# Two of four feed-forward half steps of a decoder in seven block products for eight

## The chip, the cores and the metric

One core of one Trainium2 chip runs the whole program, in one launch. The metric is device time in microseconds (us), the median of three runs. The engines are TensorE (PE in the profile; PEld is its load of weights), VectorE (DVE), ScalarE (ACT), GpSimd (POOL) and SyncE (SP), which here only issues transfers. TensorE multiplies out of SBUF into PSUM, which has eight banks of 2 KB on each of 128 partitions.

## What is computed

The trunk has two layers, 544 tokens (512 of a prompt and 8 x 4 of a sample group), a model width of 1024 and a feed-forward width of 2816. Each layer has a feed-forward half step, a mixer (an mLSTM in layer 0, a chunk MLP in layer 1) and a second half step; a norm ends it. All is float32.

```python
def _swiglu(x, w_gate, w_up, w_down):
    return (jax.nn.silu(x @ w_gate) * (x @ w_up)) @ w_down
...
    for i in range(DEPTH):
        x = x + 0.5 * _swiglu(_rmsnorm(x, p['norm_ff1'][i]),
                              p['ffn1_w_gate'][i], p['ffn1_w_up'][i], p['ffn1_w_down'][i])
...
        x = x + out
        x = x + 0.5 * _swiglu(_rmsnorm(x, p['norm_ff2'][i]),
                              p['ffn2_w_gate'][i], p['ffn2_w_up'][i], p['ffn2_w_down'][i])
    y = _rmsnorm(x, p['norm_final'])
```

The half steps are called ffn1,0, ffn2,0, ffn1,1 and ffn2,1 here, in the order of their running.

## The kernel before, in words

Features lie on the partitions: x is eight tiles of 128 x 544, and a weight is used in pieces of 128 x 1024, eight blocks of 128 x 128 that make one tile of 128 outputs. The tokens go in two halves of 272 columns, one PSUM bank each.

A float32 product is three products of a narrower format (float32r). Each operand is split exactly into a part `hi` and a part `lo` (`split_into`): ScalarE copies it into the narrower format (`whi` for weights, `hh` for the hidden activations, `xgh` for x), VectorE subtracts that copy from it (`wlo`, `hl`, `xgl`). `mm3` then adds hi times hi, hi times lo and lo times hi for every k block and both halves: 48 matmuls for eight k blocks, all recorded at L191. `whi` and `wlo` have two buffers each, the loaded pieces (`raw`) six.

A half step (`ffn`) takes the 22 hidden tiles in groups of 8, 8 and 6 (`FF_GROUPS`). For each hidden tile j it makes the gate product, then the up product; VectorE multiplies the gate by the norm's factors (L277), ScalarE takes Silu (L278), GpSimd multiplies by the factors again (L279), VectorE multiplies by the up product (L180), and the result is split into `hh` and `hl`. Behind a group come eight down products of 48 or 36 matmuls, each added to one tile of x (L294). In the last group of a half step each new x tile is at once scaled, split and squared for the next norm (`prep`); the squares are added up by GpSimd (L234). `prep_end` turns the sum into the norm's factors `rstd` through TensorE, a square root on ScalarE (L245) and a reciprocal on VectorE (L246). The program's last group goes through `last_down` (its products of the last tile at L319, its update of x at L323) and `finish`, the final norm.

At the start the x tiles and the first piece of weights come in, interleaved; the splits of x go ahead of the squares, which VectorE adds, and the factors are made behind the first two products.

The order on each engine is made by a list scheduler when the program is built; each engine then works its queue strictly in that order, and waits on semaphores of the others. Weights are issued by SP, one transfer of 512 KB for a piece.

## Time and profile before

| what | us |
|---|---|
| median of three runs | 2337.63 (2336.07 to 2338.55) |
| span of the profiled execution, first to last instruction | 2334.9 |
| TensorE busy | 2314.8 (99%) |
| VectorE busy | 1126.5 (48%) |
| ScalarE busy | 787.8 (34%) |
| GpSimd busy | 351.5 (15%) |

A time of the runs holds what lies ahead of the first and behind the last instruction too, so it stands 2.7 us above the span. A busy time is the length of all instructions of an engine with overlaps counted once; matmuls overlap each other, so the mean length of one (288 ns) is over twice the distance from one to the next.

### The profile page before, as it was taken

To read this page: it belongs to the slowest core of one execution; us is meant where nothing else is said; L and a number is where in the kernel's file an instruction comes from. 1 tells how busy PE (TensorE), PEld (TensorE's weight loads), DVE (VectorE), ACT (ScalarE), POOL (GpSimd) and SP (SyncE) were. 2 spreads that over 40 slices of the span, in tenths; PEclk is the share of its full clock that TensorE was granted. 3 is DMA by queue.
4 is the path that set the end of the run, shared out by engine and by line. 5 is a ranking of instruction groups with operands and counts; after the bars stand their busy time and mean duration, and the time that the engine had idled before them with its cause. 6 is when DMAs were issued, how large, how long until landed. Compare 5 with 4: busy or idle time off the path is not lost.

```text
span 2334.9 us, 42078 instructions
## 1 busy us (share of the span) xinstructions
PE 2314.8 (99%) x18076; PEld 2220.8 (95%) x18076; DVE 1126.5 (48%) x1642; ACT 787.8 (34%) x1066; POOL 351.5 (15%) x403
## 2 busy tenths in 40 slices
PE   8999999999999999999999999999999999999998
PEld 8999999988987789999999999999999999999998
DVE  5333336543456676644454454545444644333334
ACT  5222123434455453422222342122233433222123
POOL 1101013332111100210111121011121121001011
PEclk9999999999999999999999999999999999999999
DMA  5322223467767663547563444746333223223221
GB/s 179 90 83 91 91 76 110 152 223 233 247 214 259 237 192 102 173 157 265 157 212 118 139 148 157 264 157 210 119 102 96 70 82 91 90 83 91 91 71 59
DMA packets 131089, 337.50 MB, mean 145 GB/s; under 512 B 13168, under 2 KB 26304, under 8 KB 130904
## 3 DMA queue, kind: packets, MB, share of 16 engines
q1 hardware_dynamic: 101152, 276.52, 36.7%
q0 software_dynamic: 9200, 34.02, 4.5%
q10 hardware_dynamic: 20552, 24.29, 2.9%
q8 instruction: 142, 2.33, 0.4%
q14 instruction: 43, 0.35, 0.0%
HBM read 274.97 MB, written 59.81 MB: 143 GB/s over the span
## 4 chain that ended last, share of the span: by engine, by line
PE 95%; DVE 2%; DMA 2%; ACT 1%; issue 0%; POOL 0%; SPq 0%; DVEq 0%; ACTq 0%
PE mm L191 83%; PE mm L926 2%; PE s L191 2%; PE s L719 1%; PE s L497 1%; PE s L853 1%; PE s L889 1%; PE s L1110 1%; DMA xs<-xsd 1%; DMA raw<-in_ml_down 1%; PE s L1040 0%; PE s L836 0%; DVE wlo L206 0%; PE s L478 0%; DVE wg L424 0%
## 5 line engine op out<-in xcount | busy, mean ns | idle before, releaser
L205 ACT ACTIVATE whi<-raw 128x1024 fp32r<-128x1024 f32 (+2 forms) x345 | 358.0, 1038 | 1296.1 <-PE mm L191 1114.4
L191 PE MATMUL mm<-xgh,whi 128*128 128x272 f32 x3744 | 779.7, 289 | 5.8 <-ACT whi L205 5.8
L191 PE MATMUL mm<-xgl,whi 128*128 128x272 f32 x3744 | 776.1, 288 | 0.4 <-DVE xgl L209 0.4
L191 PE MATMUL mm<-xgh,wlo 128*128 128x272 f32 x3744 | 775.1, 288 | 0.0
L191 PEld LDWEIGHTS mm<-xgh,whi 128*128 128x128 f32 x3744 | 588.3, 188 | 23.8 <-issue 14.1
L191 PEld LDWEIGHTS mm<-xgl,whi 128*128 128x128 f32 x3744 | 587.8, 188 | 0.7 <-DVE xgl L209 0.6
L191 PEld LDWEIGHTS mm<-xgh,wlo 128*128 128x128 f32 x3744 | 587.4, 188 | 0.5 <-issue 0.5
L206 DVE TENSOR_TENSOR wlo<-raw,whi 128x1024 fp32r<-128x1024 f32 (+2 forms) x345 | 413.5, 1199 | 63.0 <-ACT whi L205 49.2
L191 PE MATMUL mm<-hh,whi 128*128 128x272 f32 x1508 | 314.2, 289 | 1.3 <-DVE x L294 1.3
L191 PE MATMUL mm<-hl,whi 128*128 128x272 f32 x1508 | 312.2, 288 | 0.0
L191 PE MATMUL mm<-hh,wlo 128*128 128x272 f32 x1508 | 312.0, 288 | 0.1
L279 POOL TENSOR_TENSOR s<-s,rstd 128x544 f32<-128x544 f32 x88 | 151.8, 1726 | 1002.5 <-ACT s L278 1002.5
L191 PEld LDWEIGHTS mm<-hh,whi 128*128 128x128 f32 x1508 | 236.2, 188 | 6.2 <-issue 6.1
L191 PEld LDWEIGHTS mm<-hh,wlo 128*128 128x128 f32 x1508 | 236.5, 188 | 0.8 <-DVE wlo L206 0.8
L191 PEld LDWEIGHTS mm<-hl,whi 128*128 128x128 f32 x1508 | 236.8, 188 | 0.0
L180 DVE TENSOR_TENSOR t<-mm,s 128x544 f32<-128x544 f32 x83 | 60.1, 725 | 331.6 <-PE mm L191 331.6
L294 DVE SCALAR_TENSOR_TENSOR x<-mm,x 128x544 f32<-128x544 f32 x88 | 63.7, 724 | 249.1 <-PE mm L191 249.1
L277 DVE TENSOR_TENSOR t<-mm,rstd 128x544 f32<-128x544 f32 x88 | 63.6, 724 | 240.5 <-PE mm L191 240.4
L1114 DVE SCALAR_TENSOR_TENSOR c<-c,gib,s 128x512 f32<-128x512 f32 x128 | 88.1, 740 | 0.0
L234 POOL TENSOR_TENSOR acc<-acc,sq 128x544 f32<-128x544 f32 x35 | 56.5, 1614 | 175.7 <-ACT sq L233 175.7
L206 DVE TENSOR_TENSOR hl<-t,hh 128x544 fp32r<-128x544 f32 x88 | 63.2, 718 | 2.9 <-ACT hh L205 2.9
L1116 POOL DMA_DIRECT2D out_Cs<-c x32 | 25.0, 782 | 253.4 <-DVE c L1114 246.6
(304 smaller groups left out, 1763.1 us busy)
## 6 DMA issues: line engine op xcount, KB each, us to landing
raw<-in_ffn_up SPq DMA_DIRECT2D x88, 512.0 KB
raw<-in_ffn_gate SPq DMA_DIRECT2D x87, 512.0 KB
raw<-in_ffn_down SPq DMA_DIRECT2D x64, 512.0 KB
c<-in_sC SPq DMA_DIRECT2D x64, 512.0 KB
c<-in_sC SPq DMA_DIRECT2D x32, 1024.0 KB
out_Cs<-c POOLq DMA_DIRECT2D x32, 1024.0 KB, 6.0
raw<-in_ml_up SPq DMA_DIRECT2D x32, 512.0 KB
raw<-in_ffn_down SPq DMA_DIRECT2D x32, 384.0 KB
```

The source lines that it names most:

```text
L180: self.nc.vector.tensor_tensor(out=self.v2(out), in0=ps[:, :, :HN], in1=self.v2(by), op=ALU.mult)
L191: nc.tensor.matmul(out=ps[h], lhsT=w[:, wsl], rhs=x[:, h * HN:(h + 1) * HN], start=k == 0 and q == 0, stop=k == n - 1 and q == 2)
L205: nc.scalar.activation(out=hi, in_=src, func=AF.Copy)
L206: nc.vector.tensor_tensor(out=lo, in0=src, in1=hi.bitcast(F32), op=ALU.subtract)
L234: (eng or nc.gpsimd).tensor_tensor(out=self.acc, in0=self.acc, in1=sq, op=ALU.add)
L277: nc.vector.tensor_tensor(out=self.v2(t), in0=psg[:, :, :HN], in1=self.v2(self.rstd), op=ALU.mult)
L279: nc.gpsimd.tensor_tensor(out=s, in0=s, in1=self.rstd, op=ALU.mult)
L294: nc.vector.scalar_tensor_tensor(out=xv, in0=ps[:, :, :HN], scalar=0.5, in1=xv, op0=ALU.mult, op1=ALU.add)
L497: nc.tensor.matmul(out=ps[:, tt * P:(tt + 1) * P], lhsT=t[:, tt * P:(tt + 1) * P], rhs=wd[w], start=True, stop=True)
L926: nc.tensor.matmul(out=ps, lhsT=kk[:, tt], rhs=vv[:, tt], start=tt == 0 and q == 0, stop=tt == 3 and q == 2)
L1114: nc.vector.scalar_tensor_tensor(out=c0[:, r, :], in0=c0[:, r, :], scalar=self.gib[:, h, b:b + 1], in1=ps[r], op0=ALU.mult, op1=ALU.add)
L1116: nc.gpsimd.dma_start(out=self.pair(o["Cs"], v)[:, h, dsl].rearrange("r p e -> p r e"), in_=c0)
```

## The change

ffn1,0 and ffn2,1 use the scheme of Strassen and Winograd. A weight is cut into blocks of 2 x 2: two neighbouring k tiles by two neighbouring output tiles; the tokens' two halves are the second matrix's columns. Seven products of block sums then stand for eight of blocks. `sums` makes the sums of x (once) or of the hidden activations on VectorE, in a tile of eight slots of 272 columns (`hT`), and splits seven of them. `weight_sums` loads the four blocks of a weight's piece once, in four transfers of 256 KB, and forms four sums: two on GpSimd (L396, L399), two on VectorE (L397, L398). It splits the seven blocks in three pieces of 128 x 1024 (`whi`, `wlo`, as before with two buffers) and one of 128 x 512 (`whd`, `wld`, one buffer).

`seven` makes the products in four PSUM banks of one tile `set` (two such tiles, all eight banks), P1 to P7 in the order of the code: P1 in bank 0, P2 in bank 1, P3 on bank 2, P4 on bank 0, P5 on bank 3, P6 on bank 2, P7 on bank 1. Between them ScalarE carries a bank's content to another: L425 behind P1 (bank 0 to bank 2, negated), L428 behind P2 (bank 1 to SBUF, `e`), L430 behind P3 (bank 2 to bank 3), L433 behind P5 (bank 3 to bank 1, negated). A product has 12 matmuls of 272 columns in a gate or up seven; in a down seven it has 9, or 6 in the last group, since the hidden tiles go in pairs, in groups of three, three, three and two (`SV_GROUPS`). All these matmuls are recorded at L421. A gate seven is followed by L458 to L460 on VectorE, Silu of 1088 columns (L461) and a product on GpSimd of 1088 columns (L462), an up seven by L467, L469 and L470 and the sums of the hidden pair (L353, L355, L356, then the split of 1904 columns into `hh` and `hl` at L241 and L242), a down seven by L493, L495 and L496, which add to two tiles of x.

The program has 72 sevens: 44 for gate and up, 28 for down. The last group of ffn2,1 goes through a rewritten `last_down` in the old scheme, with 24 matmuls a tile. At the start all of x is summed and split pair by pair through one buffer of `hT`, and GpSimd adds the squares. The middle stages keep their code; their buffers are grouped otherwise (`x_pool`, `psum`).

```diff
+SEVEN = {("ffn1", 0), ("ffn2", 1)}
+SV_GROUPS = ((0, 3), (3, 6), (6, 9), (9, 11))
+ADDS = "eng"
+B11, B21, B22, T4, T1, T2, T3, B12 = range(8)
...
     def prep(self, k):
+        if self.xkind == "s":
+            if k % 2:
+                self.px[k // 2] = self.sums_x(k - 1)
+            self.prep_sq(k)
+            return
...
+    def set(self):
+        return self.pp.tile([P, 4, 512], F32, tag="set", name="set", bufs=2)
+
+    def sums(self, t, hi, lo, parts=1):
+
+        nc = self.nc
+        nc.vector.tensor_tensor(out=t[:, T1:T3 + 1:2], in0=t[:, B12:B12 + 1].to_broadcast([P, 2, HN]),
+                                in1=t[:, B11:B22 + 1:2], op=ALU.subtract)
+        nc.vector.tensor_tensor(out=t[:, T2], in0=t[:, B22], in1=t[:, T1], op=ALU.subtract)
+        nc.vector.tensor_tensor(out=t[:, T4], in0=t[:, B21], in1=t[:, T2], op=ALU.subtract)
+        for c in ((slice(0, 7),) if parts == 1 else (slice(0, 3), slice(3, 7))):
+            self.split_into(hi[:, c], lo[:, c], t[:, c])
+        return hi, lo
+
+    def sums_x(self, k):
+
+        nc = self.nc
+        t = self.ht.tile([P, 8, HN], F32, tag="hT", name="hT", bufs=1)
...
+        return self.sums(t, hi, lo, 2)
+
+    def weight_sums(self, src):
...
+        ta, tb, tc = (raw(self.wp, "raw", 2, RAW) for _ in range(3))
+        td = raw(self.wx, "rawd", 1, 2)
+        nc.sync.dma_start(out=ta[:, 0], in_=b11)
...
+            t21 = raw(self.wx, "raw21", 1, 1)
+            nc.sync.dma_start(out=t21[:, 0], in_=b21)
+            nc.sync.dma_start(out=tc[:, 0], in_=b22)
+            nc.sync.dma_start(out=tb[:, 0], in_=b12)
+            nc.gpsimd.tensor_tensor(out=ta[:, 1], in0=ta[:, 0], in1=t21[:, 0], op=ALU.add)
+            nc.vector.tensor_tensor(out=tc[:, 1], in0=tc[:, 0], in1=t21[:, 0], op=ALU.add)
+        nc.vector.tensor_tensor(out=tb[:, 1], in0=tc[:, 1], in1=ta[:, 0], op=ALU.add)
+        nc.gpsimd.tensor_tensor(out=td[:, 0], in0=tb[:, 1], in1=tb[:, 0], op=ALU.add)
+        out = []
+        for t in (ta, tb, tc):
+            hi, lo = (self.wp.tile([P, 2, 512], F32R, tag=g, name=g, bufs=WSP)[:, :, :n] for g in ("whi", "wlo"))
+            self.split_into(hi, lo, t)
+            out += [(hi[:, i], lo[:, i]) for i in range(2)]
+        hi, lo = (self.wx.tile([P, 512], F32R, tag=g, name=g, bufs=1)[:, :n] for g in ("whd", "wld"))
+        self.split_into(hi, lo, td[:, 0])
+        return out + [(hi, lo)]
+
+    def seven(self, t, src, xs, scale=1.0, sums=None):
...
+        w11, w7, w12, w6, w22, w5, w3 = self.weight_sums(src)
+        bank = [t[:, b, :HN] for b in range(4)]
...
+        product(0, w11, B11, True)
+        nc.scalar.activation(out=bank[2], in_=bank[0], func=AF.Copy, scale=-1.0)
+        product(1, w7, T3, True)
+        e = self.wx.tile([P, HN], F32, tag="e", name="e", bufs=2)
+        nc.scalar.activation(out=e, in_=bank[1], func=AF.Copy, scale=scale)
+        product(2, w6, T2, False)
+        nc.scalar.activation(out=bank[3], in_=bank[2], func=AF.Copy)
+        product(0, w12, B21, False)
+        product(3, w5, T1, False)
+        nc.scalar.activation(out=bank[1], in_=bank[3], func=AF.Copy, scale=-1.0)
+        product(2, w22, T4, False)
+        product(1, w3, B22, False)
+        return e.unsqueeze(1).to_broadcast([P, 2, HN])
+
+    def ffn_seven(self, name, l, nextc, start=False):
...
+                    t = self.set()
+                    e = self.seven(t, gate[j], xs)
...
+                    u = self.set()
...
+                    e = self.seven(u, up[j], xs)
+                    h = ht.tile([P, 8, HN], F32, tag="hT", name="hT", bufs=1)
...
+                    hs.append(self.sums(h, hi, lo))
...
+                    e = self.seven(t, down[m][:, :, j0:j1], hs, scale=0.5)
```

How the built order moves. In the order's rows a name's number is that of its buffer, and a semaphore is named by the engine or queue that raises it.

TensorE before, inside a gate product of ffn1,0 (`mm_309` is its PSUM tile, `xgh_`/`xgl_` the tiles of x, `whi_305`/`wlo_306` the piece of weights):

```order
L191 MATMUL mm_309<-xgh_121,whi_305 128x272 x2
L191 MATMUL mm_309<-xgl_122,whi_305 128x272 x2
L191 MATMUL mm_309<-xgh_121,wlo_306 128x272 x2
L191 MATMUL mm_309<-xgh_125,whi_305 128x272 x2
L191 MATMUL mm_309<-xgl_126,whi_305 128x272 x2
```

TensorE now, in an up seven of ffn1,0 (`set_1748` are its four banks, `set_1883` those of the gate seven behind it, `xsh_`/`xsl_` the sums of x): the last two matmuls of P1 and the first three of P2, then, further on, the last of P5, the next seven's first two, and the first of P6.

```order
L421 MATMUL set_1748<-xsl_180,whi_1767 128x272
L421 MATMUL set_1748<-xsh_179,wlo_1768 128x272
L421 MATMUL set_1748<-xsh_125,whi_1771 128x272 [waits Activation_49]
L421 MATMUL set_1748<-xsl_126,whi_1771 128x272
L421 MATMUL set_1748<-xsh_125,wlo_1772 128x272 [waits DVE_49]
```

```order
L421 MATMUL set_1748<-xsh_179,wlo_1776 128x272
L421 MATMUL set_1883<-xsh_125,whi_1897 128x272 [waits Activation_49]
L421 MATMUL set_1883<-xsl_126,whi_1897 128x272
L421 MATMUL set_1748<-xsh_125,whi_1775 128x272 [waits Activation_49]
L421 MATMUL set_1748<-xsl_126,whi_1775 128x272
```

Before, the row of matmuls had no wait; now P2 and P6 each begin with a wait on a semaphore of ScalarE (that of P2 is raised by L425, that of P6 by L433).

ScalarE before, in the same half step, one hidden tile after another:

```order
L205 ACTIVATE whi_547<-raw_545 128x1024 [waits DMAHW0_49,PE_49,Activation_49]
L278 ACTIVATE s_536<-t_535 128x544 [waits DVE_49,Pool_49]
L205 ACTIVATE whi_602<-raw_600 128x1024 [waits DMAHW1_49,PE_49,Activation_49]
L205 ACTIVATE hh_541<-t_535 128x544 [waits DVE_49]
L205 ACTIVATE whi_667<-raw_665 128x1024 [waits DMAHW2_49,PE_49,Activation_49]
L278 ACTIVATE s_656<-t_655 128x544 [waits DVE_49,Pool_49]
```

ScalarE now, in the same up seven (`set_1748`): from its first copy to the one behind P5.

```order
L425 ACTIVATE set_1748<-set_1748 128x272 [waits PE_49]
L241 ACTIVATE whi_1775<-raw_1756 128x1024 [waits DMAHW0_49,DVE_49,PE_49]
L461 ACTIVATE s_1747<-s_1747 128x1088 [waits DVE_49]
L428 ACTIVATE e_1808<-set_1748 128x272 [waits PE_49,Activation_49]
L430 ACTIVATE set_1748<-set_1748 128x272 [waits PE_49,Activation_49]
L241 ACTIVATE whi_1897<-raw_1884 128x1024 [waits DMAHW3_49,PE_49,Pool_49]
L433 ACTIVATE set_1748<-set_1748 128x272 [waits PE_49,Activation_49]
```

Before, weight splits took turns with Silu and the split of a hidden tile; now the third weight split (`whi_1775`) and the Silu of the gate seven before it stand between L425 and L428, and the next seven's first split stands ahead of L433.

VectorE before, behind the last up product of a group (`t_1135` is the hidden tile, `x0_77` the first tile of x):

```order
L277 TENSOR_TENSOR t_1135<-mm_1031,rstd_277 128x544 [waits PE_49]
L206 TENSOR_TENSOR wlo_1148<-raw_1145,whi_1147 128x1024 [waits DMAHW3_49,Activation_49]
L180 TENSOR_TENSOR t_1135<-mm_1086,s_1136 128x544 [waits PE_49,Pool_49]
L206 TENSOR_TENSOR wlo_1204<-raw_1201,whi_1203 128x1024 [waits DMAHW4_49,Activation_49]
L206 TENSOR_TENSOR hl_1142<-t_1135,hh_1141 128x544 [waits Activation_49]
L294 SCALAR_TENSOR_TENSOR x0_77<-mm_1151,x0_77 128x544 [waits PE_49]
```

VectorE now, behind the last up seven of a group (`hT_2127` holds the hidden pair's sums; the rows of `raw_2343` and `wld_2165` belong to the weights of the down sevens):

```order
L467 TENSOR_TENSOR hT_2127<-set_2003,s_2002 128x2x272 [waits PE_49,Pool_49]
L469 TENSOR_TENSOR hT_2127<-set_2003,e_2063 128x544
L242 TENSOR_TENSOR wld_2165<-rawd_2142,whd_2164 128x384 [waits Activation_49]
L470 TENSOR_TENSOR hT_2127<-hT_2127,s_2002 128x544 [waits DVE_49]
L397 TENSOR_TENSOR raw_2343<-raw_2343,raw21_2346 128x384 [waits DMAHW4_49,DMAHW1_49]
L353 TENSOR_TENSOR hT_2127<-hT_2127 128x2x272 [waits DVE_49]
L355 TENSOR_TENSOR hT_2127<-hT_2127 128x272 [waits DVE_49]
L356 TENSOR_TENSOR hT_2127<-hT_2127 128x272 [waits DVE_49]
L242 TENSOR_TENSOR hl_2132<-hT_2127,hh_2131 128x1904 [waits Activation_49]
```

Before, two operations and a split of 544 columns led from the last up product to the group's down products; now seven operations on the pair and a split of 1904 columns lead there, with two on weights in between.

## Rows read from the trace of the kernel before

**Rows 1.** The page: span, busy time by engine, the chain by engine and by line
```profile
span 2334.9 us, 42078 instructions
...
PE 2314.8 (99%) x18076; PEld 2220.8 (95%) x18076; DVE 1126.5 (48%) x1642; ACT 787.8 (34%) x1066; POOL 351.5 (15%) x403
...
PE 95%; DVE 2%; DMA 2%; ACT 1%; issue 0%; POOL 0%; SPq 0%; DVEq 0%; ACTq 0%
```

**Rows 2.** Stretches: us, busy time of each engine, granted clock, DMA share, GB/s
```profile
200.00:300.00 100.00, 100.00 (x796) 100.00 (x795) 35.34 (x39) 23.65 (x26) 7.11 (x4) 1.00 0.29 88
2322.00:2327.00 5.00, 3.48 (x25) 2.95 (x24) 2.78 (x8) 0.98 (x4) 2.32 (x4) 0.94 0.00 0
2327.00:2335.00 8.00, 0.79 (x2) 0.00 (x0) 2.34 (x6) 0.41 (x1) 2.86 (x4) 0.50 0.83 279
```

**Rows 3.** Timeline of VectorE in ffn1,0: start, length, operation
```profile
202.16 0.72 DVE L180 TENSOR_TENSOR t<-mm,s 128x544 f32<-128x544 f32 x1 [3.98 <-PE mm L191]
...
214.21 0.72 DVE L180 TENSOR_TENSOR t<-mm,s 128x544 f32<-128x544 f32 x1 [3.98 <-PE mm L191]
```

**Rows 4.** Timeline of TensorE, last product, half of the tokens
```profile
2317.15 0.28 PE L319 MATMUL mm<-hh,whi 128*128 128x256 f32 x1
...
2317.27 0.28 PE L319 MATMUL mm<-hl,whi 128*128 128x256 f32 x1
```

**Rows 5.** Timeline, end of a down product and its reader
```profile
2312.37 0.41 PE L191 MATMUL mm<-hh,wlo 128*128 128x272 f32 x2
...
2312.82 0.73 DVE L323 SCALAR_TENSOR_TENSOR x<-mm,x 128x544 f32<-128x544 f32 x1 [2.26 <-PE mm L191]
```

**Rows 6.** ScalarE by line and shape: busy, mean ns, idle ahead
```profile
L205 ACT ACTIVATE whi<-raw 128x1024 fp32r<-128x1024 f32 x311 | 329.7, 1060 | 1220.6 <-PE mm L191 1068.3 <-issue 75.5 <-DMA raw<-in_ml_up 27.3
...
L205 ACT ACTIVATE whi<-raw 128x768 fp32r<-128x768 f32 x32 | 27.0, 844 | 75.5 <-PE mm L191 46.0 <-issue 29.3
...
L245 ACT ACT_TABLE_LOAD x6 | 7.7, 1283 | 0.1
...
L245 ACT ACTIVATE rstd<-s,eps 128x272 f32<-128x272 f32 x12 | 5.2, 484 | 0.1
...
L358 ACT ACTIVATE rs<-s 128x288 f32<-128x288 f32 x1 | 0.4, 411 | 2.1 <-PE s L354 2.1
L358 ACT ACTIVATE rs<-s 128x256 f32<-128x256 f32 x1 | 0.4, 366 | 0.0
```

**Rows 7.** Timeline, a wait of TensorE for a weight split
```profile
13.29 1.22 DVE L206 TENSOR_TENSOR wlo<-raw,whi 128x1024 fp32r<-128x1024 f32 x1
...
14.56 0.52 PE L191 MATMUL s<-xgh,wlo 128*128 128x272 f32 x2
```

**Rows 8.** VectorE by line and shape
```profile
L206 DVE TENSOR_TENSOR wlo<-raw,whi 128x1024 fp32r<-128x1024 f32 x311 | 381.0, 1225 | 62.7 <-ACT whi L205 48.9
...
L206 DVE TENSOR_TENSOR hl<-t,hh 128x544 fp32r<-128x544 f32 x88 | 63.2, 718 | 2.9 <-ACT hh L205 2.9
...
L246 DVE RECIPROCAL rstd<-rstd 128x272 f32<-128x272 f32 x12 | 21.4, 1824 | 3.5 <-ACT rstd L245 3.5
```

**Rows 9.** Timeline of TensorE at the start
```profile
6.84 0.66 PE L191 MATMUL mm<-xgh,wlo 128*128 128x272 f32 x2
...
8.67 0.46 PE L191 MATMUL mm<-xgh,whi 128*128 128x272 f32 x2
...
20.20 0.42 PE L191 MATMUL mm<-xgh,whi 128*128 128x272 f32 x2
```

**Rows 10.** Timeline of VectorE and GpSimd behind the mLSTM
```profile
943.43 0.79 DVE L209 SCALAR_TENSOR_TENSOR xgl<-x,cols,xgh 128x544 fp32r<-128x544 f32 x1 [0.56 <-ACT xgh L208]
...
948.42 1.88 DVE L209 SCALAR_TENSOR_TENSOR xgl<-x,cols,xgh 128x544 fp32r<-128x544 f32 x1
...
939.15 1.37 POOL L234 TENSOR_TENSOR acc<-acc,sq 128x544 f32<-128x544 f32 x1 [0.31 <-ACT sq L233]
...
948.14 1.57 POOL L234 TENSOR_TENSOR acc<-acc,sq 128x544 f32<-128x544 f32 x1 [2.70 <-ACT sq L233]
```

More of the change, by code (lines that the diff above doesn't have):

```diff
@@ L1 @@
+import contextlib
 import numpy as np
@@ L1144, in run @@
             nc.vector.memset(self.eps, EPS)
-            late = com.tile([P, 1], F32, name="late")
-            nc.scalar.activation(out=late, in_=self.eps, func=AF.Copy)
             self.mhalf = com.tile([P, 4], F32, name="mhalf")
```

208 lines of the change are left out of this document (162 added, 46 removed).

## The prediction

> **What bounds the kernel now.** I read the page's busy shares and its chain first: TensorE is busy 99% of the span, and 95% of the chain that ended last is TensorE [rows 1]. In a stretch of a feed-forward half step it is busy 100.00 of 100 us at a granted clock of 1.00, that is 2.4 GHz, while VectorE has 35, ScalarE 24 and GpSimd 7 [rows 2]. So a matmul taken away is worth its cadence, and a stall put into TensorE's queue costs its full length. The cadence: two VectorE readings of successive up products stand 12.05 us apart and hold 96 matmuls [rows 3], so 0.1255 us for one of 272 columns. One half of the tokens by itself, in the order the sevens use, goes no slower (0.12 at 256 columns) [rows 4].
>
> **What it removes.** A gate or up product of a pair of hidden tiles falls from 96 matmuls to 84, a down product from 72 to 63, those of the last group of ffn1,0 from 48 to 42. With the odd ones at both ends 746 of 17608 go, by the built order: 93.6 us, if TensorE stays fed. The order says that it does not.
>
> **What it adds: hand-overs inside a seven.** The built order shows that each of P2, P3, P4 and P6 waits for the ScalarE copy ahead of it (P2 for L425, P3 for L428, P4 for L430, P6 for L433), and each copy waits for the last matmul of the product before. P2 needs no data of L425; they share the tile of four banks, and that is enough. One round trip has four parts. (a) From the start of a product's last matmul to the start of its reader: the matmul pair of 2312.37 has its second at 2312.495, the reader starts at 2312.82, so 0.325 [rows 5]. (b) The copy of 272 columns out of PSUM: 0.366 at 256 and 0.411 at 288 columns, so 0.39; a square root of 272 took 0.484, the upper end [rows 6]. (c) From an engine's end to TensorE's start: 13.29 + 1.22 = 14.51 to 14.56, so 0.05. (d) The restart: the pair that started there took 0.52 where its like took 0.41, so 0.11 [rows 7]; it may be nothing here. Less the 0.1255 that passes anyway: **0.75 us for one hand-over**. Ahead of P6 stand two matmuls of the next seven, so 0.50 there.
>
> **The copy that comes late.** ScalarE's queue has the third weight split between L425 and L428, since `whi` has two buffers and the third split overwrites the first, whose last reader is P2's 11th matmul of 12. It takes 1.06 [rows 6]. So L428 starts not at P2's end but after it: 0.325 + 1.06 + 0.39 + 0.05 + 0.11 - 0.25 = 1.69 for the stall before P3. In the up seven the Silu of 1088 columns stands there too: by the slope of the 768 and 1024 rows (0.844 ns a column) 1.11 more, 2.80. In a down seven the split has 768 columns (0.844): 1.47; with 512, 0.63: 1.25.
>
> **The sevens.**
> - Gate: 84 x 0.1255 = 10.54, and 0.75 + 1.69 + 0.75 + 0.50 = 3.69. Up: 10.54 and 4.80. The pair 29.57 against 24.10: +5.47 x 22 = **+120.4**.
> - Down of three pairs: 7.91 + 3.47 = 11.38 against 9.04: +2.34 x 24 = **+56.2**.
> - Down of two: 5.27 + 3.25 = 8.52 against 6.02: +2.50 x 4 = **+10.0**. The next norm's copies and squares stand in ScalarE's queue there: about 1.8 x 3 = **+5.4**.
>
> **Group changes.** The first down product of a group needs the last hidden pair's sums. After that pair's up seven, VectorE's queue holds L467, L469, L470 and L353 (0.72 each), a split and an add of 384 columns (0.55 each), L355 and L356 (0.43 each), then ScalarE's split of 1904 columns (1.80), then VectorE's (2.15), at 1.056 ns a column by its 544 and 1024 rows [rows 8]. With 0.33 to the first of them and some 0.1 to 0.2 of hops that is 9.4 us. TensorE has six matmuls, 0.75, to lay over it. Before, 42 matmuls (5.3 us) covered a chain of 544 columns. +8.8 x 7 = **+61.6**; last_down's is in the seams.
>
> **Start.** Before, the third product starts at 20.20; less its 96 predecessors this is work without a gap from 8.15 [rows 9]. Now the squares are summed by GpSimd in front of ScalarE's `sqh`: seven adds of 1.4 (as the 939.15 row, alone [rows 10]) to 1.7 and two weight adds end near 20. Behind `sqh`, in one queue, come the third pair's copies, a table load (1.28), two roots; VectorE's two reciprocals (1.82 each) stand before the third pair's last split, which frees `hT` for the fourth. That pair's copies then start near 30, its last split ends near 36.6. TensorE has done 21 matmuls, 2.6 us, so its work is as if without a gap from about 34: +25.7, with waits on first weights **+27** (+10 if GpSimd isn't the limit).
>
> **Clock.** After the start the pairs of 6.84 to 8.67 come 0.46 apart, 0.229 a matmul, for twelve matmuls, though the granted clock reads 1.00 there; where TensorE idled at the end it reads 0.50, 1.2 GHz [rows 2, 9]. If each idle of 9 us brings that back, 12 x 0.1035 = 1.24, **+8.7** for seven.
>
> **Seams.** Entering ffn2,1 through sums (two copies, L353 to L356 and the last splits, 5.3 us by the slopes above, where one tile's 0.66 and 0.72 stood), last_down's first wait, two tiles' norm at the way out: 4 + 4 + 2 = **+10**, the last two estimated from the same chains.
>
> **What costs nothing.** Per pair of sevens VectorE has 6 x 1.225 + 2 x 0.68 + 4 x 0.68 + 7 x 0.72 + 2 x 0.43 + 2.15 = 19.5 us, ScalarE 13.7, both inside 29.57. GpSimd's adds and product are 4 x 1.29 + 2.74 = 7.9 by the 939.15 row. VectorE waits beside GpSimd: an operation of 0.79 took 1.88 beside one of 1.57, so 1.09 was lost of 1.57 [rows 10]; by that share 24.9 us are needed, at worst the sum, 27.4. That still lies under 29.57. The Trainium skill ("SBUF — State Buffer", section "Who interferes with whom") says that a VectorE instruction with two SBUF inputs contends with GpSimd's reads and that the second to come is wholly blocked; the row agrees nearly, and by the rule it would be the 27.4. This speaks against the change: 24.9 to 27.4 is more than the 24.10 of before. The cover is 2 us by the worst case; each us missing costs 22. SP issues eight loads of 256 KB for two of 512 KB a pair of products: 2 MB in 29.6 us, 71 GB/s against the 88 of before [rows 2].
>
> **Sum**, on the profiled execution: span 2334.9 [rows 1], 2.7 around it, which makes the median of the runs shown, 2337.6. 120.4 + 56.2 + 10.0 + 5.4 + 61.6 + 27 + 8.7 + 10 = 299.3: **2637 us**.
>
> **Rivals.**
> - *Faster: the hand-overs are hidden*, since the sequencer starts P2 ahead of the copy's end or the copy is short. A pair of sevens saves 3.02 us; over eight waits this decides at 0.38 us for each mean hand-over. Then 2337.6 - 93.6 + 27 + 10 = about 2281. Against it: the waits stand in the built order, the copy alone is 0.37 to 0.48 [rows 6], and VectorE with GpSimd needs 24.9 (slower again). 3%.
> - *Only the round trips cost*: the third split and the Silu are not in L428's way. Saves (0.94 + 2.05) x 22 + 0.72 x 28 = 86: 2551. For it: were `whi` free earlier it would be so; against it, ScalarE's queue is in order. 8%.
> - *The clock falls inside the sevens*: TensorE pauses for 0.5 to 2.8 us four times in 15 us. At 0.229 a matmul all 5376 in the sevens cost 0.1035 more, +556: 3193; a part of the time, anything between. For it: where the last products have gaps 0.94 is granted, and 0.50 near idle [rows 2]; against it: that 0.94 is near full at a busy share of 70% (3.48 of 5.00), the 71% that I forecast for a pair of sevens (21.08 of 29.57). The Trainium skill ("TensorE: Matmul & The Clock Gate", section "A second HAM failure mode: psum-queue depth-cycling") tells of a kernel whose short idles between groups of matmuls let the clock swing. 10%.
> - *The change doesn't do what it says*: nothing for it, the count of matmuls falls in the built order.
>
> **Numbers.** The forecast has 79%. Its own range: no restart cost -32 (288 hand-overs by 0.11), copies of 0.366 or 0.484 -7 or +27, group changes and seams 20 either way, start -17, clock -9; VectorE late by 1 us in each pair +22. Together 2565 to 2715. To leave out no more than two in ten it reaches to the second rival below and some way into the third above: 2540 to 2745. A measurement of this kernel tells 0.2%, some 4.7 us, from no change. Faster is the first rival alone, 3%; within 0.2% needs hand-overs near 0.38, 1%; slower 96%.
>
> **What would show it.** TensorE busy near 88% of the span, its idle released by L425, L428, L430 and L433 in about 0.75, 1.7 to 2.8, 0.75 and 0.5 us; sevens of 14.2, 15.3 and 11.4 us; some 9 us idle before `hl` of 1904 columns at seven group changes; steady products from about 34 us; the middle stages as long as before; a granted clock near 1.00 in the sevens. A clock well under 1 there, waits on `wlo` or `hl` inside the sevens, or no idle before P2, would make it wrong.

## The result, and the profile of the changed kernel

The changed kernel takes **2732.52 us** (median of four runs, 2726.67 to 2742.65) beside 2337.33 of the kernel before in the same rounds: a ratio of 1.1696, 95% interval 1.1671 to 1.172. It is slower by 395 us, where 299 had been forecast; the time lies in the stated range, 95 us above the point, but above the forecast's own range of 2565 to 2715, in the stretch that had been added for the rival of the falling clock. The profiled execution took 2730.85, with a span of 2729.1.

The page of the changed kernel, busy time and the chain that ended last, to be read against [rows 1]:

```profile
span 2729.1 us, 42433 instructions
...
PE 2399.8 (88%) x17336; PEld 2229.1 (82%) x17336; DVE 1524.6 (56%) x2087; ACT 1023.7 (38%) x1486; POOL 536.0 (20%) x532
...
PE 81%; ACT 7%; DVE 5%; issue 4%; DMA 3%; POOL 0%; ACTq 0%; POOLq 0%; DVEq 0%
```

TensorE has 740 instructions less and is busy 85 us longer, over a span that is 394 us longer. Its busy share fell from 99% to 88%, as forecast; what was not forecast is that its busy time rose. Matmuls at half clock, 68 us of them counted below, are a part of that; the rest was not followed up.

Stretches of the changed kernel (columns as in [rows 2]): ffn1,0 behind its start, the middle stages, ffn2,1, then the stretch of [rows 2], a piece of a gate seven with its P3, one of the up seven behind it, and the first group change:

```profile
40.00:626.00 586.00, 441.79 (x2766) 402.31 (x2767) 338.39 (x389) 222.91 (x339) 130.25 (x88) 0.88 0.21 61
626.00:2147.00 1521.00, 1510.87 (x11707) 1419.49 (x11705) 815.20 (x1278) 554.80 (x782) 255.62 (x340) 1.00 0.52 171
2147.00:2729.00 582.00, 439.90 (x2844) 402.05 (x2844) 337.52 (x391) 222.79 (x334) 129.97 (x87) 0.88 0.21 61
...
200.00:300.00 100.00, 77.55 (x532) 71.42 (x530) 64.82 (x69) 39.38 (x56) 29.31 (x17) 0.94 0.21 62
...
207.00:219.00 12.00, 9.81 (x72) 9.16 (x72) 6.18 (x7) 4.82 (x8) 1.79 (x2) 1.00 0.22 68
...
219.00:231.00 12.00, 8.81 (x44) 8.27 (x45) 6.86 (x7) 4.09 (x6) 4.59 (x3) 0.72 0.22 66
...
149.00:166.00 17.00, 12.48 (x48) 10.89 (x49) 5.16 (x5) 3.88 (x7) 1.00 (x1) 0.51 0.09 24
```

The clock is 0.88 in both half steps of sevens and 1.00 between them, where TensorE is busy 99% as before. In the stretch of [rows 2] 796 matmuls became 532. The gate's piece has the full clock, the up's 0.72, the group change 0.51. By the last update of x, ffn1,0 takes 626.4 us instead of 410.2 (+216), the middle 1520.6 instead of 1513.0 (+8), ffn2,1 582.1 instead of 411.7 (+170).

What TensorE waited for in the changed kernel (us in total, times, the longest):

```profile
PE set L421 <- ACT e L428: 116.8, 72, 3.7
PE set L421 <- ACT hh L241: 46.6, 7, 7.0
PE set L421 <- ACT set L430: 38.8, 72, 0.8
PE set L421 <- ACT set L425: 33.9, 71, 1.0
PE set L421 <- ACT whi L241: 22.8, 5, 16.5
PE set L421 <- ACT set L433: 13.7, 48, 0.5
PE set L421 <- DVE hl L242: 11.1, 7, 1.6
PE set L421 <- ACT xsh L241: 6.9, 2, 6.4
PE s L285 <- DVE sql L242: 5.7, 1, 5.7
PE set L421 <- DVE wlo L242: 5.5, 2, 3.6
```

The four copies release TensorE 72, 72, 71 and 48 times in 72 sevens, 203 us in all, and `hh` and `hl` seven times each, once for each group change. Waits on `wlo` are two.

One up seven on ScalarE, then the same on TensorE (start, length, operation, in brackets the idle time ahead and what ended it):

```profile
218.92 0.38 ACT L425 ACTIVATE set<-set 128x272 f32<-128x272 f32 x1 [0.68 <-PE set L421]
221.04 1.06 ACT L241 ACTIVATE whi<-raw 128x1024 fp32r<-128x1024 f32 x1 [1.74 <-PE set L421]
222.01 1.09 ACT L461 ACTIVATE s<-s 128x1088 f32<-128x1088 f32 x1
223.01 0.38 ACT L428 ACTIVATE e<-set 128x272 f32<-128x272 f32 x1
226.42 0.38 ACT L430 ACTIVATE set<-set 128x272 f32<-128x272 f32 x1 [3.03 <-PE set L421]
```

```profile
219.36 0.39 PE L421 MATMUL set<-xsh,whi 128*128 128x272 f32 x1 [0.47 <-ACT set L425]
219.59 0.29 PE L421 MATMUL set<-xsl,whi 128*128 128x272 f32 x1
219.71 0.29 PE L421 MATMUL set<-xsh,wlo 128*128 128x272 f32 x1
...
223.44 0.39 PE L421 MATMUL set<-xsh,whi 128*128 128x272 f32 x1 [2.30 <-ACT e L428]
223.67 0.39 PE L421 MATMUL set<-xsl,whi 128*128 128x272 f32 x1
223.85 0.43 PE L421 MATMUL set<-xsh,wlo 128*128 128x272 f32 x1
224.08 0.43 PE L421 MATMUL set<-xsh,whi 128*128 128x272 f32 x1
```

The third `whi` and the Silu stand ahead of L428, as the built order had them. P2's matmuls follow each other by 0.125 us; P3's, behind an idle of 2.30 us, from the third on by 0.227: half clock.

A group change on TensorE, from the last matmul that needs no sum of the third pair to the return of the clock:

```profile
143.09 0.28 PE L421 MATMUL set<-hh,wlo 128*128 128x272 f32 x1
149.82 0.59 PE L421 MATMUL set<-hh,whi 128*128 128x272 f32 x1 [6.45 <-ACT hh L241]
151.99 0.60 PE L421 MATMUL set<-hl,whi 128*128 128x272 f32 x1 [1.58 <-DVE hl L242]
...
153.29 0.60 PE L421 MATMUL set<-hh,whi 128*128 128x272 f32 x1 [0.47 <-ACT set L425]
...
165.50 0.37 PE L421 MATMUL set<-hh,whi 128*128 128x272 f32 x1
165.71 0.29 PE L421 MATMUL set<-hl,whi 128*128 128x272 f32 x1
```

From 143.09 to 151.99 are 8.9 us: the chain of sums that had been put at 8.8 net. Then the matmuls stand 0.227 apart until 165.5, where 12 of them, 1.24 us, had been forecast.

### The profile page after: what moved, and what is told of

It is laid out like the page before. It is cut to its first block, busy times and chain, and to the rows that moved or that the text cites. A ratio compares the mean times of both kernels' runs of the same rounds, so it can differ in the third digit from the quotient of the medians.

```text
span 2729.1 us, 42433 instructions
## 1 busy us (share of the span) xinstructions
PE 2399.8 (88%) x17336; PEld 2229.1 (82%) x17336; DVE 1524.6 (56%) x2087; ACT 1023.7 (38%) x1486; POOL 536.0 (20%) x532
## 4 chain that ended last, share of the span: by engine, by line
PE 81%; ACT 7%; DVE 5%; issue 4%; DMA 3%; POOL 0%; ACTq 0%; POOLq 0%; DVEq 0%
PE mm L227 44%; PE set L421 26%; PE mm L1141 2%; DVE wlo L242 2%; PE s L934 1%; ACT whi L241 1%; PE s L1068 1%; PE s L1104 1%; ACT set L430 1%; PE s L712 1%; ACT e L428 1%; ACT s L461 1%; ACT set L433 1%; PE s L227 1%; PE mm L525 1%
## 5 line engine op out<-in xcount | busy, mean ns | idle before, releaser
L241 ACT ACTIVATE whi<-raw 128x1024 fp32r<-128x1024 f32 (+2 forms) x432 | 429.8, 995 | 1100.9 <-PE mm L227 639.8
L242 DVE TENSOR_TENSOR wlo<-raw,whi 128x1024 fp32r<-128x1024 f32 (+2 forms) x432 | 519.5, 1204 | 423.7 <-ACT whi L241 410.3
L227 PE MATMUL mm<-xgh,whi 128*128 128x272 f32 x2368 | 494.8, 290 | 0.2 <-DVE x L1175 0.2
L227 PE MATMUL mm<-xgl,whi 128*128 128x272 f32 x2368 | 490.7, 288 | 0.3 <-DVE xgl L245 0.3
L421 PE MATMUL set<-xsh,whi 128*128 128x272 f32 x1056 | 345.0, 327 | 165.4 <-ACT e L428 82.7
L227 PE MATMUL mm<-xgh,wlo 128*128 128x272 f32 x2368 | 489.8, 288 | 0.0
L421 PEld LDWEIGHTS set<-xsh,whi 128*128 128x128 f32 x1056 | 218.2, 207 | 207.8 <-ACT e L428 92.6
L227 PEld LDWEIGHTS mm<-xgl,whi 128*128 128x128 f32 x2368 | 371.6, 188 | 0.6 <-DVE xgl L245 0.5
L421 PE MATMUL set<-xsh,wlo 128*128 128x272 f32 x1056 | 324.4, 307 | 5.5 <-DVE wlo L242 5.5
L421 PE MATMUL set<-xsl,whi 128*128 128x272 f32 x1056 | 324.6, 307 | 1.4 <-DVE xsl L242 1.4
L421 PE MATMUL set<-hh,whi 128*128 128x272 f32 x480 | 172.2, 359 | 115.4 <-ACT hh L241 46.6
L421 PEld LDWEIGHTS set<-hh,whi 128*128 128x128 f32 x480 | 108.2, 225 | 144.6 <-ACT hh L241 48.2
L421 PEld LDWEIGHTS set<-xsh,wlo 128*128 128x128 f32 x1056 | 219.2, 208 | 6.4 <-DVE wlo L242 6.1
L421 PEld LDWEIGHTS set<-xsl,whi 128*128 128x128 f32 x1056 | 220.1, 208 | 1.7 <-DVE xsl L242 1.7
L399 POOL TENSOR_TENSOR rawd<-raw 128x512 f32<-128x512 f32 (+2 forms) x72 | 99.1, 1376 | 438.3 <-DMA raw<-in_ffn_down 213.2
L421 PE MATMUL set<-hl,whi 128*128 128x272 f32 x480 | 158.7, 331 | 11.1 <-DVE hl L242 11.1
L396 POOL TENSOR_TENSOR raw<-raw,raw 128x512 f32<-128x512 f32 (+2 forms) x72 | 97.0, 1348 | 312.4 <-DMA raw<-in_ffn_down 91.4
```

The costliest lines, as they stand in the source:

```text
L227: nc.tensor.matmul(out=ps[h], lhsT=w[:, wsl], rhs=x[:, h * HN:(h + 1) * HN], start=k == 0 and q == 0, stop=k == n - 1 and q == 2)
L241: nc.scalar.activation(out=hi, in_=src, func=AF.Copy)
L242: nc.vector.tensor_tensor(out=lo, in0=src, in1=hi.bitcast(F32), op=ALU.subtract)
L396: nc.gpsimd.tensor_tensor(out=ta[:, 1], in0=ta[:, 0], in1=t21[:, 0], op=ALU.add)
L399: nc.gpsimd.tensor_tensor(out=td[:, 0], in0=tb[:, 1], in1=tb[:, 0], op=ALU.add)
L421: nc.tensor.matmul(out=bank[b], lhsT=ww[:, c], rhs=xx[:, i], start=start and z == 0, stop=z == last, skip_group_check=True)
```

## The experiments

Versions that build on one another; all times are medians of runs beside the kernel before on the same chip (2335.9 to 2336.8). The line numbers of a version's profile can differ by a few from those of the changed kernel.

| run | built on | us | ratio to before, 95% interval |
|---|---|---|---|
| e1_third_later | change | 2632.71 | 1.1272 (1.1255 to 1.1288) |
| e2_own_banks | change | 2437.79 | 1.0439 (1.0423 to 1.0454) |
| e3_banks_third | e2 and e1 | 2453.88 | 1.0504 (1.0488 to 1.052) |
| e4_adds_by_dma | change | 2755.83 | 1.1783 (1.1762 to 1.1804) |
| e5_gate_ahead | e2 | 2406.61 | 1.0301 (1.0287 to 1.0315) |
| e7_last_only | e5 | 2348.64 | 1.0046 (1.0032 to 1.006) |
| e8_norm_first | e7 | 2340.49 | 1.0017 (1.0009 to 1.0026) |
| e9_cover_entry | e8 | 2334.70 | 0.9991 (0.9982 to 1.0) |
| e10_cover_dma | e9 | 2413.76 | 1.0326 (1.0312 to 1.034) |
| e11_two_buffers | e9 | 2337.40 | 1.0001 (0.9992 to 1.001) |
| e12_two_pools | e9 | 2329.37 | 0.9969 (0.9957 to 0.9981) |

**The third split behind L428.** It and the Silu leave L428's way; P2's last matmul now reads the high part that the split overwrites, so that the split can only come behind P2.

```diff
-        for t in (ta, tb, tc):
+        def two(t):
...
+        out = two(ta) + two(tb)
...
+        return out + [(hi, lo)], lambda: two(tc)
...
-                for ww, xx in ((w[0], xh), (w[0], xl), (w[1], xh)):
+                for ww, xx in ((w[0], xh), (w[1], xh), (w[0], xl)) if b == 1 else ((w[0], xh), (w[0], xl), (w[1], xh)):
...
         nc.scalar.activation(out=e, in_=bank[1], func=AF.Copy, scale=scale)
+        w22, w5 = third()
```

> The changed kernel with the third weight split of each seven formed behind the copy L428 instead of ahead of it, in ScalarE's queue (P2's last matmul now reads the high part, so the split becomes free only with P2's end; the Silu moves behind the copy too). Hand-over theory: P3's pause falls from 1.69 (gate), 2.80 (up) and 1.47 (down) to the 0.75 of the other hand-overs, in all 0.94 x 22 + 2.05 x 22 + 0.72 x 24 + 0.5 x 4 = 85 us. If the half clock inside the up sevens comes from that longest pause, their 27 us of slow matmuls go too and some of the downs': 2610 to 2625, no clock below 1.00 in gate and up sevens. Rival, the clock falls with TensorE's busy share and not with the longest pause: the slow matmuls stay, near 2650. Rival, VectorE with GpSimd sets the period of a pair (25 to 27 us): the pair falls from 31.4 only to what that allows and new waits on wlo or whi appear, above 2680.

2632.71, 100 us less, between the 2610 to 2625 of the hand-over theory and the 2650 of the rival. Its waits of TensorE:

```profile
PE set L421 <- ACT e L428: 44.2, 72, 2.5
PE set L421 <- ACT set L431: 41.3, 72, 1.9
...
PE set L421 <- DVE wlo L242: 14.3, 25, 3.6
```

The wait on L428 is 73 us shorter, that on `wlo` 9 longer, that on L431 (L430 in the change) 2.5 longer: 61 net. Counting the matmuls on TensorE's timeline that follow their predecessor by the half-clock distance, not directly behind a pause, the loss to the half clock went from 68 to 32 us, 36 less; together 97 of the 100. The idle ahead of P3 fell from 2.31 to 0.55 us in the up sevens (medians of 22), and from 273 such matmuls in them none is left; that of the gates fell from 1.31 to 0.55. So the stall ahead of P3 cost twice, by itself and by the clock behind it. The longest pause of a seven and the sum of its pauses fell together here, so which of them the clock followed stays open.

**Each bank a tile of its own.** The four copies then hand over only what a product needs; the readers of the set become one operation for each bank.

```diff
-        return self.pp.tile([P, 4, 512], F32, tag="set", name="set", bufs=2)
+        return [self.pp.tile([P, 512], F32, tag=f"set{b}", name=f"set{b}", bufs=2) for b in range(4)]
...
-                    nc.vector.tensor_tensor(out=s[:, 0], in0=t[:, 0:2, :HN], in1=r2, op=ALU.mult)
+                    for b in range(2):
+                        nc.vector.tensor_tensor(out=s[:, 0, b], in0=t[b][:, :HN], in1=r2[:, b], op=ALU.mult)
```

> The changed kernel with each of the four PSUM banks of a seven a tile of its own; VectorE's operations that read two banks at once become two of 272 columns. Hand-over theory: P2, P4 and P6 no longer wait for copies that they don't need, P3, P5 and P7 wait for copies that lie a whole product back; a gate or up seven comes to 10.5 to 11.5 us, a down one to 8 to 9, group changes and start stay (some 100 us over before with their slow clock), total 2430 to 2470. Rival, VectorE (20.1 us a pair now) with GpSimd's 7.9 binds: a pair takes 25.5 to 28, the down sevens 8.7, total 2490 to 2540, and TensorE's waits name wlo, whi or hl. Rival, TensorE's pauses are something else than the shared tile: little changes, 2700.

2437.79: 295 of the 395 us are back. Waits of TensorE, a stretch, and three forms of VectorE:

```profile
PE set L421 <- DVE wlo L242: 35.7, 28, 3.2
PE set L421 <- ACT hh L241: 30.5, 7, 5.0
...
PE set L421 <- ACT set L430: 21.2, 14, 2.3
...
PE set L421 <- ACT set L425: 5.4, 8, 1.9
```

```profile
200.00:300.00 100.00, 89.06 (x662) 86.60 (x663) 84.94 (x109) 47.72 (x73) 28.93 (x20) 0.95 0.29 85
```

```profile
L397 DVE TENSOR_TENSOR raw<-raw,raw 128x512 f32<-128x512 f32 x44 | 53.4, 1214 | 25.1 <-issue 11.4 <-DMA raw<-in_ffn_up 9.4 <-DMA raw<-in_ffn_gate 2.4
...
L242 DVE TENSOR_TENSOR wld<-rawd,whd 128x512 fp32r<-128x512 f32 x44 | 44.6, 1014 | 0.0
...
L398 DVE TENSOR_TENSOR raw<-raw 128x512 f32<-128x512 f32 x44 | 34.5, 784 | 1.0
```

No wait on L428 is left among the longest, and those on L425 are 8. In their place stand 28 waits on `wlo`, and VectorE is busy 85 of 100 us. Its operations with two operands in SBUF meet GpSimd's at other places now (an operation of GpSimd lies over 17 of these 44 L397 and 3 of the L398, 9 and 15 in the change): L397 takes 1214 ns (744 in the change) and `wld` 1014 (735), but L398 784 (1331), so that the three together grew by only 0.20 us. A gate and an up seven take 12.6 and 11.7 us (means of the distances between their L425s, group changes apart), the pair 24.3 beside 24.10 before; the hand-over theory had put each at 10.5 to 11.5, so the total was met with longer sevens than expected.

**Both edits**, with the split of a hidden pair behind the next seven's L433 where it is not the group's last.

```diff
+        w22, w5 = third()
...
+        if self.later:
+            self.later()
+            self.later = None
...
-                    hs.append(self.sums(h, hi, lo))
+                    hs.append((hi, lo))
+                    self.sums(h)
+                    def split(h=h, hi=hi, lo=lo):
+                        self.split_into(hi, lo, h[:, :7])
```

> Both edits: own banks, and the third weight split and the Silu behind the copy of P2, the split of a hidden pair formed as late as the next seven's last copy allows. Hand-over theory: as own banks alone, less what is left of waits behind the long splits, 2400 to 2450; the saving of the two edits doesn't add up, since with own banks nothing but P7 hangs on L428. Rival, VectorE with GpSimd binds: no faster than own banks alone, 2490 to 2540.

2453.88, 16 more than with the banks alone: no faster, as the rival had said, though its 2490 to 2540 was not reached. TensorE's waits on `wlo` rose to 46.4 us in 44. So the hand-over behind L428 no longer binds; the waits point to VectorE, which the version with less work for it, further down, tests.

**The weights' adds in accumulating transfers** in the changed kernel, so that VectorE and GpSimd do less.

```diff
-ADDS = "eng"
+ADDS = "dma"
```

> The changed kernel with two of the four weight sums of each seven formed by transfers that add (the kernel's own other setting) instead of by GpSimd and VectorE; the hand-overs are as they were. Hand-over theory: the sums are off the path, within 15 us of the changed kernel, 2715 to 2745. Rival, VectorE with GpSimd sets the period: two adds of 0.7 to 1.3 fewer on each, 50 to 90 us faster. Third way: the added transfers (six and two for four) come late and put waits on whi on TensorE, slower than 2760.

2755.83, 23 more. Its waits on L430 are 53.9 us and on `wlo` 21.6 in 16; GpSimd takes 0.85 to 0.90 us (means) to issue an accumulating transfer. Less work for VectorE brought nothing here, but the later transfers added waits of their own, so that the run alone does not rule VectorE out; the first experiment, 100 us faster with the same work for VectorE, does.

**The next group's first gate seven ahead of the down sevens**, on top of the banks, so that a product without hidden sums covers the group change.

```diff
+            def ahead(j):
+                t = self.set()
+                e = self.seven(t, gate[j], xs)
...
-                    t = self.set()
-                    e = self.seven(t, gate[j], xs)
...
+                    s, u = todo or ahead(j)
+                    todo = None
...
+                if not lastg:
+                    todo = ahead(j1)
```

> Own banks as before, and the next group's first gate seven put ahead of a group's down sevens, so that it lies over the chain that makes the last hidden pair's parts; the last group of each half step has no such cover. If TensorE's pauses are what own banks still pay at group changes (40 us of waits on hh and hl at seven changes, and some 11 us of matmuls at the half clock behind them), six of seven go: some 45 us off, 2385 to 2400. Rival: with own banks VectorE, 84% busy beside GpSimd, is the bound, and uses TensorE's pauses to work off what it is behind; then the waits move to wlo and the gain is under 25 us, 2415 to 2435.

2406.61, 31 less, between the two. The stretch again:

```profile
200.00:300.00 100.00, 91.40 (x709) 89.25 (x707) 91.46 (x115) 54.74 (x83) 33.45 (x22) 1.00 0.29 88
```

The waits on `hh` fell from 30.5 to 4.5 us and the clock is at 1.00, but VectorE is busy 91.5 of 100 us, and a pair of sevens inside a group takes 25.0 in the median (a gate mostly 12.1 to 12.6, an up 12.5 to 12.9). That lies between the 24.9 and 27.4 that the prediction had worked out for VectorE beside GpSimd: with the cover that it spoke of gone, the work that it covered seems to bind.

**Sevens in ffn2,1 alone**, ffn1,0 and the start as before.

```diff
-SEVEN = {("ffn1", 0), ("ffn2", 1)}
+SEVEN = {("ffn2", 1)}
```

> The same, with ffn2,1 alone in sevens; ffn1,0 and the start as in the kernel before. With own banks ffn1,0 took 66 us longer than before and ffn2,1 31, the stages between 9. If the costs of the two half steps are their own, this gives 31 less what the gate seven ahead saves in one half step (10 to 20) over before: 2345 to 2358. Rival: the start and the way into the mLSTM are not what makes ffn1,0 dearer, then half of all that own banks pay stays, 2370 to 2390.

2348.64, 11 to 12 us over the kernel before and inside the 2345 to 2358 expected: one half step in sevens, with everything above, still loses.

**The norm's factors multiplied into x ahead of its sums.** Then gate and up products need no factors: two operations on VectorE and one on GpSimd go from every pair, and the sums wait for the factors.

```diff
-        nc.scalar.activation(out=t[:, B11:B12 + 1:B12 - B11], in_=self.v2(self.x[k]), func=AF.Copy,
-                             scale=self.col(self.pc + k))
...
+            nc.vector.scalar_tensor_tensor(out=o, in0=self.v2(self.x[k + i]), scalar=self.col(self.pc + k + i),
+                                           in1=self.v2(self.rstd), op0=ALU.mult, op1=ALU.mult)
...
-                nc.gpsimd.tensor_tensor(out=s.rearrange("p a b c -> p a (b c)"),
-                                        in0=s.rearrange("p a b c -> p a (b c)"),
-                                        in1=self.rstd.unsqueeze(1).to_broadcast([P, 2, NT]), op=ALU.mult)
```

> The same as the one before, with the norm's factors multiplied into x ahead of the sums (VectorE, once), so that a pair of sevens has no products with the factors any more: VectorE 1.6 us less a pair, GpSimd 2.6 less, ScalarE takes Silu from PSUM. The way in gets longer, since the sums wait for the factors: about 9 us for them and some 20 for four pairs in one buffer, against 5 now. If VectorE with GpSimd bounds a pair with own banks, a pair falls from 24 to 21.5 to 22.5, 11 pairs: 15 to 28 us off and 20 to 25 on, 2335 to 2360. Rival: the pair doesn't get shorter, because waits and not the work bound it: 2365 to 2385.

2340.49. Two stretches, the entry into ffn2,1 and the sevens behind it:

```profile
1926.00:1946.00 20.00, 6.53 (x16) 3.75 (x16) 16.00 (x19) 6.79 (x8) 0.22 (x1) 0.56 0.10 26
...
2000.00:2100.00 100.00, 96.39 (x758) 95.20 (x757) 87.91 (x114) 57.55 (x93) 28.47 (x21) 1.00 0.34 95
```

With less for VectorE and GpSimd to do the sevens run with TensorE 96% busy and at full clock, 10.5 us an up and 11.7 to 12.4 a gate, a pair of 22.2 to 22.9. So their work did set the pair, and which of the two engines' was not separated. But the entry is empty: the sums of x come one pair behind another through one buffer, from 1923 to 1957 us.

**The first hidden pair by whole products**, which need no sums, as cover for the entry.

```diff
+            def plain(w, i, t):
...
+            plain(gate[0], 0, t)
             self.prep_end([u[2][:, :HN], u[3][:, :HN]])
+            plain(gate[0], 1, t)
...
             xs = [self.sums_x(2 * k) for k in range(KD // 2)]
```

> The kernel with the norm ahead of the sums, and the first hidden pair of ffn2,1 by whole products as in the kernel before (192 matmuls, 24 us), which need only x without the factors and lie over the factors and the sums of x. In the run before it the way in kept TensorE idle or at half speed from 1923 to 1957, some 30 us; VectorE still needs 9 us for the factors, 22 for the sums and 5 for weight parts, so about 10 to 12 us of waiting stay, and the whole pair costs 2 us more than a pair of sevens: 15 to 20 us off, 2319 to 2327, 0.4 to 0.7% below the kernel before. Rival: the sums get later, since VectorE has the whole products' parts to form as well, and nothing is gained: 2335 to 2345.

2334.70, next to the rival's 2335 to 2345 and not the 2319 to 2327 expected: TensorE is full from 1926 to 1946 now, but busy only 12.71 us of 25 from 1950 to 1975, at 0.53, and the first seven's L422 (L425 in the change) comes at 1969.9.

**The same with accumulating transfers**, `ADDS` as above.

> The kernel before it with two of the four weight sums formed by transfers that add (the setting that made the changed kernel 23 us slower, where TensorE's queue was full of pauses). Here a pair of sevens still leaves TensorE 3 to 4 of 100 us idle, with VectorE 87% busy, part of it beside GpSimd. If VectorE and GpSimd are the bound, two adds fewer on each in a seven take the 3 to 4% away (some 7 to 10 us of 240) and shorten the way in by 2 to 3: 2322 to 2328. Rival: the transfers that add need two landings one behind the other and are issued by GpSimd, and what they bring late costs more: 2340 to 2360.

2413.76, 79 more, far beyond the rival's 2340 to 2360 too. TensorE waits 55.2 us for `wlo` (20 times, up to 4.7) while VectorE is busy only 185 of the 300 us from 2000: the two transfers of a piece stand one behind the other, and each lands 4.1 to 5.0 us (medians) after GpSimd issued it.

**Two buffers for the sums**, with one instead of two for GpSimd's block `rawd`, for room, and the plain pair's product on VectorE.

```diff
-        t = self.ht.tile([P, 8, HN], F32, tag="hT", name="hT", bufs=1)
+        t = self.ht.tile([P, 8, HN], F32, tag="hT", name="hT", bufs=2)
...
-        td = raw(self.wx, "rawd", 1, 2)
+        td = raw(self.wx, "rawd", 1, 1)
```

> The kernel with the covered way in (e9), with two buffers for the sums of x instead of one, and the plain pair's product with the factors on VectorE instead of GpSimd. In e9 VectorE's two products of the first pair took 3.76 instead of 1.48 us beside GpSimd's 3.00, its other operations of the way in lost some 3 us more beside GpSimd, and each pair of sums waited 1.2 us for ScalarE in the one buffer, with TensorE at half speed from 1952 to 1972. Both edits shorten VectorE's way from the factors to the last sums by 2.3 - 1.2 + 4 to 6 us: TensorE is fed again 6 to 9 us earlier, 2325 to 2329, 0.3 to 0.5% below the kernel before. Rival: the other buffer only lets VectorE run ahead, the last sums come no earlier: 2332 to 2337.

2337.40, nothing gained. The first seven comes 8.4 us earlier, at 1961.5, but the gates behind a group change take 14.7 to 15.0 us instead of 12.2, and this wait is 15.5 us where the run before had 7.9:

```profile
PE set L420 <- ACT set L429: 15.5, 9, 2.6
```

**The second buffer in a pool that is closed again**, so that `rawd` keeps its two; the plain pair's product is on VectorE here too, and the two are not told apart.

```diff
-        t = self.ht.tile([P, 8, HN], F32, tag="hT", name="hT", bufs=1)
+        t = (self.ht2 if k % 4 else self.ht).tile([P, 8, HN], F32, tag="hT", name="hT", bufs=1)
...
+            with self.pool("ht2", side="left") as self.ht2:
+                xs = [self.sums_x(2 * k) for k in range(KD // 2)]
```

> The kernel of the covered entry with a second buffer for the pairs' sums in a pool that is closed again, so that the two raw buffers for GpSimd's blocks stay, and the plain pair's product on VectorE. The run with two sums buffers came to the entry about 8 us earlier and lost it to gates of 14.5 to 15 us with one raw buffer. If those two things are apart, this one keeps the gates at 11.7 to 12.3 us and takes the 8 us: 2326 to 2330. Rival, the entry's sums are still bound by VectorE beside GpSimd, whatever buffers there are: 2332 to 2337, the time of the covered entry.

**2329.37**, a ratio of 0.9969 with an interval under 1: 7 us below the kernel before, and the one version whose interval lies under 1. Its entry:

```profile
1950.00:1975.00 25.00, 16.52 (x66) 13.77 (x67) 22.48 (x31) 10.22 (x13) 2.62 (x2) 0.66 0.16 44
```

The first seven comes at 1961.8, 8.1 earlier than with the covered entry; the first gate behind it takes 16.7 instead of 13.2 us, the gates behind a group change stay at 12.2, and 5.3 of the 8.1 us remain in the median. It has 328 matmuls less than the kernel before, 41 us at 0.1255; the entry and the pauses take 34 of them.

## Why the prediction was right, and what it mis-sized

**The mechanism was right**: TensorE's queue stops at the four copies, at the group changes and at the start, as had been said, and where the clock stayed up the sevens have the forecast length to 0.2 us. The size was not: one term was far too small, and the time lies above the forecast's own range of 2565 to 2715. (Its terms as listed come to 2552 and 2706 and not to these bounds; either way 2732.5 lies above.) That it lies in the stated range is owed to the stretch that had been added for the third rival, and its clock makes up about 60 of the 95 us. Of the signs that would make the prediction wrong one came true in part, a clock under 1 inside the sevens. Distances between the L425s of successive sevens, from ScalarE's timeline (median, mean):

| seven | forecast | median | mean | count |
|---|---|---|---|---|
| gate | 14.23 | 14.21 | 14.65 | 22 |
| up, not ahead of a group change | 15.34 | 16.46 (least 15.16) | 16.79 | 14 |
| up and group change | 24.14 | 25.53 (23.21 to 26.61) | 25.6 | 7 |
| down of three pairs | 11.38 | 11.37 to a down seven, 12.50 to a gate | 12.77 | 24 |
| down of two | 10.32 with the norm's copies | 12.20 | 12.08 | 3 |

Where the clock stayed up the forecast fits: 6 of the 14 up sevens have 15.16 to 15.22, and of the 18 down sevens with a down seven behind them the 12 that don't follow a group change 11.34 to 11.39, but for one of 13.14; the 6 that do take 14.6 to 15.8. Only the few downs of two, with the norm's copies ahead of L428, wait longer than forecast (2.2 to 2.6 us ahead of P3 in three of four). The pieces fit as well, in ScalarE's rows of the changed kernel by shape:

```profile
L241 ACT ACTIVATE hh<-hT 128x1904 fp32r<-128x1904 f32 x20 | 35.8, 1791 | 37.1 <-DVE hT L356 37.1
...
L425 ACT ACTIVATE set<-set 128x272 f32<-128x272 f32 x72 | 27.5, 382 | 58.6 <-PE set L421 58.3
...
L428 ACT ACTIVATE e<-set 128x272 f32<-128x272 f32 x72 | 27.2, 378 | 0.0
```

The copy of 272 columns took 0.38 (0.39 had been read off its neighbours in [rows 6]) and the split of 1904 columns 1.79 (1.80); the restart behind a pause cost 0.104 a time over 287 times (0.11, [rows 7]). L428 has no idle of its own at all: it was always queued behind the split.

**The step that failed is the term "Clock".** It put down +8.7, twelve slow matmuls for each group change, by the start of the kernel before [rows 9]. Measured are 689 slow matmuls, 68.3 us:
- the first down seven behind each group change, 194 of them, 19.5 us. It was 28 a change where the term had 12: what followed the idle was not a row of matmuls as at the start but a seven with pauses of its own (0.47, 1.04 and 0.53 in the rows above), and the clock came back only after some 16 us;
- the down sevens after it, 129, 12.8 us. Here the clock had mostly come back and fell anew, which no term of the sum held;
- the up sevens, 273, 27.1 us, 15 of the 22 with a piece at half clock behind the idle of 2.31 us ahead of P3. For these the prediction had a rival instead of a term, the clock that falls inside the sevens, with 10%; its price for all 5376 matmuls was 556 us, and an eighth of all matmuls of the sevens paid, these and the others of this list. What the up sevens have more there is the Silu: the gates, with 1.31 us (median of 22), kept the clock but for a few;
- gates, 81, 7.8 us, most of them in the first gate of either half step, and 12, 1.1 us, in the last matmuls ahead of the idle of the group changes.

How long a pause is does not tell by itself whether the clock falls behind it. Two neighbouring down sevens have the same pauses ahead of P2, P3 and P4, 0.47, 1.10 and 0.53 us (at 484.11, 486.58 and 488.50, and at 495.44, 497.93 and 499.84); the first keeps the clock, and behind the last pause of the second it falls to 0.50:

```profile
483.00:494.50 11.50, 9.13 (x67) 8.25 (x66) 6.77 (x10) 4.66 (x9) 2.56 (x2) 1.00 0.31 92
500.18:503.60 3.42, 3.42 (x18) 3.42 (x17) 1.06 (x2) 1.06 (x1) 0.64 (x1) 0.50 0.40 130
```

What decides between the two stays open. The argument against that rival was that 0.94 at a busy share of 70% is near full clock [rows 2]. The stretch of the changed kernel at 78% busy also reads 0.94, and holds the up seven with 0.72. A mean over a stretch says little of a clock that has two levels; the matmuls' distances say it. The Trainium skill ("TensorE: Matmul & The Clock Gate", section "A second HAM failure mode: psum-queue depth-cycling") describes a matmul kernel whose short idles between groups of matmuls let the clock go to and fro; the trace here agrees, with 0.72 granted in those 12 us, and the page weighed more than the 10% that it was given.

**Where the 95 us over the forecast are.** By the table's means: up sevens +20, gates +9, group changes +10, down sevens +33 and +5, less the 8.7 already put down: 69. The start gives +9: `sqh` came at 23.77 instead of 20, as VectorE and GpSimd each took longer beside the other (VectorE's L397 took 1.78 us, 0.74 in the mean of all), and the sums of the last pair ended late, so that TensorE waited 6.4 us for `xsh` as late as 39.77. The middle gives +8 where 2 had been put down, 6 more: 5.7 us is the wait for `sql` as the mLSTM begins. The last 11 lie at the ends of the two half steps and were not traced further. About 60 of the 95 are the clock.

**The hand-overs were the cause**: own banks bring back 295 us, and no wait on L428 remains among the longest. That P2 needs no data of L425 and waited all the same was read from the built order, and the run confirms it. The rival "only the round trips cost" had put 86 us on the third split and the Silu; the first experiment found 73 less in waits on L428, of which 11 came back in waits on `wlo` and L431, and 36 less in clock.

**The cover of VectorE** was the second thing said rightly: 24.9 to 27.4 us a pair, hidden under 29.57, a bound once the hand-overs are gone. With the cover taken away the pair took 25.0, and with less work for VectorE and GpSimd 22.2 to 22.9. The Trainium skill ("SBUF — State Buffer", section "Who interferes with whom") would have the later of the two engines wholly blocked, 27.4 us a pair if every overlap counted; measured is 25.0, near the share worked out from [rows 10], in a kernel whose operations differ from those that were added up. Single meetings are dear: with own banks L397 of 512 columns takes 0.69 us where no operation of GpSimd lies over it (27 of 44) and 2.06 in the mean where one does (17).

**The faster rival** fell as it had been argued: with nearly all of them hidden 2437.8 remain and not 2281. The group changes and the start still cost, and a pair takes 24.3, not the 21.1 of its matmuls alone.
